# A two-layer hybrid block on one core: reciprocal roots with intermediates in PSUM, other forms of two small softmax steps, and refitted costs in the list schedule

## The chip, the cores and the metric

The kernel runs on one core of a Trainium2 chip. Times are device microseconds of an execution. The core has TensorE (PE in the rows; PEld is its weight load), VectorE (DVE), ScalarE (ACT), GpSimd (POOL) and SyncE (SP), which issues the DMAs. Each works through its own list of instructions in order and waits on semaphores for the others.

## The reference

Two layers of a block over 1024 tokens of width 1024. Each layer normalizes x, projects it, and runs three mixers side by side: a sparse attention with four heads whose keys are picked by a top-256 over an index score (`dsa`), a recurrent mixer with eight heads (`rwkv7`), and an attention with a compressed, a selected and a sliding-window branch (`nsa`). Then come an output projection, a second norm and a gated feed-forward layer.

```
for l in range(DEPTH):
    mod = silu(c) @ ada_w[l] + ada_b[l]
    h = rms_norm(x, norm1_g[l]) * (1.0 + sc1) + sh1
    z = h @ w_in[l]
    ...
    mixed = concatenate([o_a, o_b, o_c]) @ w_out[l]
    x = x + g1 * mixed
    h = rms_norm(x, norm2_g[l]) * (1.0 + sc2) + sh2
    gate, up = split(h @ ffn_wi[l])
    x = x + g2 * ((silu(gate) * up) @ ffn_wo[l])
```

Reciprocal square roots occur in the norms of x, in the norms of queries and keys (over 64 columns), in the rwkv unit (length of kk) and in its group norm.

## The kernel before, in words

All is fp32. The tokens are worked on in two halves of 512 columns, features on the 128 partitions. `proj` (stage D) and `ffn` (stage F) of each layer and half are chains of dense matmuls: a weight tile arrives by DMA (`wraw`), ScalarE rounds it to `whi`, GpSimd subtracts to get `wlo`, and three 128x128x512 matmuls per tile make up an fp32 product. The order of these stages is D00, D01, F00, D10, F01, D11, F10, F11 (layer, half).

Beside them run, as generators: `index` and `topk` (the selection by bisection on the score's bits), `compress`, `att_worker` (blocks of 128 queries through `nsa` and `dsa`, both through `attend`), and `rw_worker` (16 units, one for each layer, pair of heads and half, each with 64x64 matmuls and the inversion of 16x16 blocks on VectorE in `invert16`, tile `dg`). Tiles are taken from pools: 50 `s` slots, 34 `d`, 8 `w` in SBUF, and in PSUM six banks `ps` and two banks `mm`. The sums and the cast of a norm (`ss`, `rb`) use the `mm` banks, the other sums (`ssk`) the `ps` banks.

The order of instructions is planned when the kernel is built. `Weave` runs the generators against a clock made of `cost_of` and decides which goes on; its `fits` refuses a step when the streams could no longer all get their tiles. The result is a record of instructions; `Program.order` then list-schedules every engine's queue: the earliest possible start goes first, ties by record number, with `Chip` as the model of the engines. In it an instruction with `port` set waits while the other of VectorE and GpSimd holds the port, and an instruction with an operand in PSUM does not set it. All of this happens ahead of the run; on the chip the lists are fixed.

`rsqrt` starts from an integer shift and does three Newton steps. Its named calls are `nex` (8 norms of x), `kex` (12 norms of keys and queries) and `ex` (16 rwkv units), on 128x128 tiles with x, u and y in one SBUF slot. The sums come from `sums`, four small matmuls into one PSUM bank; `cast` spreads the root back with matmuls. Its unnamed calls are on 8 to 32 columns. In `attend`, keys may lie in two runs of up to 512 columns; then the two row maxima (`m2`, `m` in the rows) and the two row sums (`s2`) are joined.

Nearly all instructions are issued from one line (L666), so the rows are told apart by tile names.

Of the kernel before, what the change touches and what calls it, by code (L numbers as in the profile page):

```python
# [13 lines left out]
F32 = mybir.dt.float32  # L14
# [206 lines left out]
class Weave:  # L221
# [39 lines left out]
    def touch(self, h):  # L261
        h.touches += 1
        if not self.plan:

            c = self.cur
            h.last = [c.step, h.tag, int(h.touches == 1)]
            h.scope = c.scope
            self.events.setdefault(c.scope, []).append(h.last)

    def done(self, h, t):  # L270
# [41 lines left out]
    def lifetimes(self):  # L312

        p = Plan()
        p.touches = {h.key: h.touches for h in self.tiles}
        p.last = {h.key: h.scope for h in self.tiles}
        for h in self.tiles:
            h.last[2] -= 1

        p.peak, p.need = {}, {}  # L320
        for scope, ev in self.events.items():
            peak = {}
            at = ev[-1][0]
            for step, tag, n in reversed(ev):
                while at > step:
                    p.peak[scope, at] = dict(peak)
                    at -= 1
                peak[tag] = max(0, peak.get(tag, 0) + n)
            for at in range(at, -1, -1):
                p.peak[scope, at] = dict(peak)  # L330
            for step, tag, n in ev:
                s = p.need.setdefault((scope, step), {}).setdefault(tag, [0, 0])
                s[0] += n
                s[1] = max(s)
        return p

    def fits(self, s):
        need = self.plan.need.get((s.scope, s.step), {})
        free = {tag: n - self.used.get(tag, 0) for tag, n in self.bufs.items()}
        if all(n[1] <= 0 for n in need.values()):  # L340
            return True
        if any(free[tag] < n[1] for tag, n in need.items()):
            return False

        rest = [(self.plan.peak.get((o.scope, o.step), {}), self.due.get(o.scope, {})) for o in self.live
                if o.step and o is not s]
# [4 lines left out]
        rest.append((self.plan.peak.get((s.scope, s.step + 1), {}), due))  # L351
        while rest:
            for r in rest:
                if all(n <= free[tag] for tag, n in r[0].items()):
                    for tag, n in r[1].items():
                        free[tag] += n
                    rest.remove(r)
                    break
            else:
                return False  # L360
        return True
# [60 lines left out]
def cost_of(key, name, aps, kw):  # L422
# [4 lines left out]
    if key == "V":  # L427
        more = 0.055 if len(aps) - acc - (name in ("scalar_tensor_tensor", "tensor_tensor", "tensor_tensor_scan",
                                                   "copy_predicated", "tensor_tensor_reduce")) > 2 else 0.0
        if name in ("tensor_reduce", "reduce_max", "reciprocal", "transpose", "tensor_tensor_reduce"):  # L430
            return 0.15 + n / 960.0 + (0.085 if acc else 0.0), False
        if acc or psum:
            return 0.15 + more + n / 960.0 + (0.085 if acc else 0.0), False
        if name in ("tensor_scalar", "tensor_copy", "memset"):
            return 0.15 + more + n / 1900.0, n > 1
        if name == "tensor_tensor_scan":
            return 0.17 + n / 487.0, True
        return 0.15 + more + n / 960.0, True
    if key == "S":
        return (0.16 if psum else 0.2) + n / 1200.0 + 0.09 * (len(aps) - 2), False  # L440
    if key == "G":
        if name == "tensor_tensor":
            return 0.18 + n / (461.0 if all(x.ap[1][0] for x in aps[1:]) else 590.0), True
        return 0.11 + n / 1220.0, name != "memset"
    a, b = aps[:2]
    plain = all(len(x.ap) <= 2 and x.ap[0][1] == 128 for x in (a, b))
# [33 lines left out]


class Rec:
    __slots__ = ("key", "name", "a", "k", "cost", "deps", "n", "users", "pe", "func", "port")


def spread(offset, dims, unit):
# [18 lines left out]
class Program:  # L505
# [32 lines left out]
    def add(self, key, name, a, k, aps, outs, cost, pe=None, port=False):  # L538
        r = Rec()
        r.key, r.name, r.a, r.k, r.cost, r.pe, r.port = key, name, a, k, cost, pe, port  # L540
        r.n, r.deps, r.users = len(self.recs), set(), []
        r.func = a[2] if key == "S" and name == "activation" else None
        wrote = {id(x) for x in outs}
        for ap in aps:
# [127 lines left out]
class Chip:  # L672
# [25 lines left out]
    def put(self, r, s):  # L698

        if r.key == "PE":  # L700
# [5 lines left out]
                self.stretch += 1  # L706
            part = rows[1] - rows[0] + cols[1] - cols[0] < 8
            more = 0.105 if not part and self.first else 0.0
            self.first = part
            share = 1.0 if not part else (rows[1] - rows[0]) * (cols[1] - cols[0]) / 16.0  # L710
            if self.slow:
                self.lost += c * (share if share > 0.3 else 0.3)
                c *= 2
            self.work += c if not part else c * max(0.3, share)
            for i in range(*rows):
                self.cells[i][cols[0]:cols[1]] = [s + c + more] * (cols[1] - cols[0])
            self.part = part
            self.free["PE"] = s + (0.007 if part else c + more)
            return s + c
        if r.key == "D":  # L720
            self.free["D"] = s + r.cost
# [28 lines left out]
def trace(ctx: ExitStack, tc: tile.TileContext, A, out, layers=L, plan=None, program=None):  # L750
# [24 lines left out]
    PT = {'mm':'mm','tm':'mm','ss':'mm','rb':'mm','xt':'mm','out':'mm'}  # L775
    PB = dict(ps=6,mm=2)
    wv = Weave({**SB, **PB}, plan)
    V, S, G, SY = (Timed(e, k, wv, program) for e, k in ((nc.vector, "V"), (nc.scalar, "S"), (nc.gpsimd, "G"), (nc.sync, "D")))
    PE = nc.tensor

# [6 lines left out]
    def slot(name, dt=F32):  # L787
        tag = SG.get(name, "s")
        name = nm(name)
        return wv.tile(tag, lambda tag: new("s", [128, 1024 if dt == BF16 else HF], dt, name, tag))  # L790
# [131 lines left out]
        eng.tensor_tensor(lo[:, :w], t[:, :w], hi.bitcast(F32)[:, :w], op=ALU.subtract)  # L922
        return hi, lo

    def rsqrt(src, w, scale, eps, clampmin=None, name=None):

        if name:
            m = slot(name)
            x, u, y = (m[:, i * 128:i * 128 + w] for i in range(3))
        else:  # L930
            x, u, y = (small(w, f"r{n}{w}", F32, 6 if w <= 16 else 1) for n in "xuy")
        if clampmin is None:
# [4 lines left out]
        V.tensor_scalar(i, x.bitcast(I32), 1, None, op0=ALU.logical_shift_right)  # L937
        V.tensor_scalar(y.bitcast(I32), i, -1.0, float(0x5F3759DF), op0=ALU.mult, op1=ALU.add)
        for _ in range(3):
            V.tensor_tensor(u, x, y, op=ALU.mult)  # L940
            V.scalar_tensor_tensor(u, u, -0.5, y, op0=ALU.mult, op1=ALU.mult)
            V.scalar_tensor_tensor(y, u, 1.5, y, op0=ALU.add, op1=ALU.mult)
        return y

# [374 lines left out]
    def proj(l, h, spills, get, lead=None):  # L1319
# [82 lines left out]
        def c_q(i):  # L1402
            def consume(ps):
# [7 lines left out]
                def post():  # L1411
# [7 lines left out]
                    qsq.append(i)  # L1419
                    if len(qsq) < 5:  # L1420
                        return
                    r = rsqrt(qsq[0][:, :128], 128, 1.0 / 64, 1e-6, name="kex")
                    yield r
                    ps = pst("ssk")
                    transpose(ps[:, :128], r)
# [343 lines left out]
    def attend(l, b, kind, q12, vcol, blocks, bias, s0, gate, po, st, final):  # L1769
# [10 lines left out]
        for hh in range(4):  # L1780
# [19 lines left out]
                    V.reduce_max(m2[:, i:i + 1], ps[:, d0:d0 + n], axis=AX.X)  # L1800
                    pss.append((ps[:, d0:d0 + n], n, None))
            if nr == 2:
                V.tensor_tensor(m2[:, 0:1], m2[:, 0:1], m2[:, 1:2], op=ALU.max)
            nb = small(1, "nb")
            V.tensor_scalar(nb, m2[:, 0:1], scl, -1.0, op0=ALU.mult, op1=ALU.mult)
            row = []
# [5 lines left out]
            yield nb if hh < 3 else None  # L1812
        rs = small(4, "rs")
        if nr == 2:
            V.tensor_tensor(rs, s2[:, :, 0], s2[:, :, 1], op=ALU.add)
            V.reciprocal(rs, rs)
        else:
            V.reciprocal(rs, s2[:, :, 0])
# [660 lines left out]
```

## Time and profile before

| what | value |
|---|---|
| median of 3 runs | 3543.34 us (3539.09 to 3548.75) |
| the profiled execution | 3547.71 us |
| its span, first to last instruction | 3545.9 us |
| PE busy | 3308.7 us (93%) |
| DVE busy | 2203.5 us (62%) |
| ACT busy | 1793.3 us (51%) |
| POOL busy | 1480.7 us (42%) |
| mean granted TensorE clock | 0.964 of full speed |

Busy time is what an engine spends in instructions, waits inside an instruction included. The share is over the whole span, and the stages differ: the windows below show which engine is nearly full in which stretch. A matmul's end is modelled, so the busy time of PE is not its peak work.

### The profile page before, as it was taken

Reading aid. Unit: us, or ns where it says so; the run is one execution under the profiler, and the core shown is the slowest. Engines: PE = TensorE matmul, PEld = TensorE weight load, DVE = VectorE, ACT = ScalarE, POOL = GpSimd, SP = SyncE. Lnnn points to the kernel's source line nnn. Section 1 sums busy time; section 2 is a strip of 40 time slices with the busy share of each in tenths; the row PEclk is TensorE's granted clock in tenths of the full one; section 3 lists DMA queues with packets and bytes.
Section 4 is the critical chain, followed back from the end, with each engine's and each line's share of the span. In section 5 each row is a group of like instructions: output and inputs, shape, how many; then the busy total and the mean of one; then the engine's idle time right before and its main releaser. Section 6 shows DMA issues by size and latency. Waiting matters only on the chain. (4 is left out here: it accounts for less than half of the span.)

```text
span 3545.9 us, 58688 instructions
## 1 busy us (share of the span) xinstructions
PE 3308.7 (93%) x20564; PEld 2488.7 (70%) x20564; DVE 2203.5 (62%) x5705; ACT 1793.3 (51%) x3712; POOL 1480.7 (42%) x1235
## 2 busy tenths in 40 slices
PE   7899898898999998989899999899899999999999
PEld 3646666666677776667677887667677777778887
DVE  4689766889898753698964112688878952151112
ACT  3445545675576463544564233557677564343222
POOL 2423443233344434452534554443343334445554
PEclk8999999988999999899899999999999999999999
DMA  8674355434722224454223333454222222433333
GB/s 281 187 244 132 88 155 145 129 98 138 240 74 86 81 88 137 128 170 115 82 71 111 98 96 116 139 163 142 68 66 85 73 70 82 126 103 98 97 96 98
DMA packets 354756, 425.00 MB, mean 120 GB/s; under 512 B 129686, under 2 KB 167190, under 8 KB 354460
## 3 DMA queue, kind: packets, MB, share of 16 engines
q1 hardware_dynamic: 354460, 421.25, 38.8%
q8 instruction: 162, 2.65, 0.3%
q14 instruction: 134, 1.10, 0.1%
HBM read 347.06 MB, written 60.44 MB: 115 GB/s over the span
## 5 line engine op out<-in xcount | busy, mean ns | idle before, releaser
L666 POOL TENSOR_TENSOR wlo<-wraw,whi 128x512 fp32r<-128x512 f32 (+1 forms) x808 | 1062.4, 1317 | 1439.0 <-ACT whi L666 1325.7
L666 ACT ACTIVATE whi<-wraw 128x512 fp32r<-128x512 f32 (+1 forms) x808 | 501.1, 621 | 980.5 <-PE mm L666 687.9
L666 PE MATMUL mm<-hh,whi 128*128 128x512 f32 x2144 | 869.8, 407 | 21.0 <-ACT whi L666 9.7
L666 PE MATMUL mm<-hh,wlo 128*128 128x512 f32 x2128 | 845.6, 397 | 7.4 <-POOL wlo L666 7.3
L666 PE MATMUL mm<-hl,whi 128*128 128x512 f32 x2112 | 840.2, 398 | 7.6 <-DVE hl L666 4.2
L666 PEld LDWEIGHTS mm<-hh,whi 128*128 128x128 f32 x2144 | 407.6, 190 | 138.7 <-issue 30.7
L666 PEld LDWEIGHTS mm<-hh,wlo 128*128 128x128 f32 x2128 | 404.9, 190 | 103.3 <-POOL wlo L666 12.9
L666 PEld LDWEIGHTS mm<-hl,whi 128*128 128x128 f32 x2112 | 402.4, 191 | 91.2 <-DVE hl L666 6.3
L666 DVE TENSOR_TENSOR sg<-sg,mm 128x512 f32<-128x512 f32 x87 | 59.6, 686 | 491.6 <-PE mm L666 489.8
L666 DVE SCALAR_TENSOR_TENSOR x<-mm,mod,x 128x512 f32<-128x512 f32 x232 | 173.1, 747 | 255.9 <-PE mm L666 255.0
L666 PE MATMUL mm<-acthi,whi 128*128 128x512 f32 x704 | 281.0, 404 | 10.9 <-ACT acthi L666 6.8
L666 PE MATMUL mm<-actlo,whi 128*128 128x512 f32 x704 | 277.8, 397 | 2.4 <-POOL actlo L666 2.2
L666 PE MATMUL mm<-acthi,wlo 128*128 128x512 f32 x704 | 276.4, 396 | 0.0
L666 ACT ACTIVATE p<-p,nb,rst 128x512 f32<-128x512 f32 (+3 forms) x256 | 170.6, 667 | 67.7 <-DVE nb L666 64.3
L666 ACT ACTIVATE junka<-score,tk_nt 128x512 int8<-128x512 f32 x240 | 166.1, 692 | 22.2 <-DVE tk_nt L666 18.5
L666 ACT COPY pT<-pt 128x512 f32<-128x512 f32 (+2 forms) x220 | 124.7, 585 | 97.5 <-PE pt L666 85.2
L666 PEld LDWEIGHTS mm<-acthi,whi 128*128 128x128 f32 x704 | 133.1, 190 | 50.4 <-ACT acthi L666 7.9
L666 PEld LDWEIGHTS mm<-actlo,whi 128*128 128x128 f32 x704 | 133.6, 190 | 32.4 <-POOL actlo L666 7.5
L666 PEld LDWEIGHTS mm<-acthi,wlo 128*128 128x128 f32 x704 | 133.6, 190 | 28.4 <-issue 0.9
L666 PE MATMUL pt<-c_ident,p 128*128 128x128 f32 x816 | 141.0, 285 | 11.1 <-DVE p L666 8.8
L666 PE MATMUL po<-pT,tm 128*64 128x256 f32 x816 | 133.1, 409 | 9.8 <-ACT pT L666 9.8
L666 DVE TENSOR_SCALAR p<-p,rs 128x512 f32<-128x512 f32 (+3 forms) x288 | 138.9, 538 | 1.2 <-DVE tk_tr L666 0.7
(384 smaller groups left out, 5979.6 us busy)
## 6 DMA issues: line engine op xcount, KB each, us to landing
wraw<-in_wi_dram SPq DMA_DIRECT2D x352, 256.0 KB, 2.6
ada<-in_ada_dram SPq DMA_DIRECT2D x192, 256.0 KB, 4.6
wraw<-in_win_dram SPq DMA_DIRECT2D x184, 256.0 KB, 3.1
wraw<-in_wo_dram SPq DMA_DIRECT2D x160, 256.0 KB, 2.6
x<-x SPq DMA_DIRECT2D x64, 256.0 KB, 4.1
w<-in_w_dram SPq DMA_DIRECT2D x64, 256.0 KB, 3.8
wraw<-in_wout_dram SPq DMA_DIRECT2D x64, 256.0 KB, 2.7
o_in<-o SPq DMA_DIRECT2D x32, 256.0 KB, 3.2
```

The costliest lines, as they stand in the source:

```text
L666: getattr(engines[r.key], r.name)(*[real(x) for x in r.a], **{n: real(x) for n, x in r.k.items()})
```

## The change

The named roots keep x and u in a PSUM bank: in columns 128 to 255 and 256 to 383 of the bank their sums lie in (argument `room`; for the queries, whose sums are added up in SBUF, the bank of the last sum). Only y stays in SBUF. In each Newton step the scalar_tensor_tensor with -0.5 comes first and the plain multiply second. In `attend` the larger of two maxima is taken by a tensor_scalar with the second as a per-partition operand, and the two sums are added by a tensor_reduce.

The rest is the planner. `cost_of` gives a VectorE memset and a strided last dimension their own rates, and judges GpSimd's operands by their last dimension; `Chip.put` lets a part-array fp32 matmul hold TensorE for half its time instead of blocking the cells it uses; and `fits` counts tiles that are taken in one stream and freed in another (`keep`) as not coming back. `prio`, `h.first` and `program.weave` only record.

```
-    def rsqrt(src, w, scale, eps, clampmin=None, name=None):
+    def rsqrt(src, w, scale, eps, clampmin=None, name=None, room=None):
         if name:
-            m = slot(name)
-            x, u, y = (m[:, i * 128:i * 128 + w] for i in range(3))
+            y = slot(name)[:, :w]
+            room = room if room is not None else src
+            x, u = (bass.AP(tensor=room.tensor, offset=room.offset + 128 * i, ap=[list(room.ap[0]), [1, w]])
+                    for i in (1, 2))
...
         for _ in range(3):
-            V.tensor_tensor(u, x, y, op=ALU.mult)
-            V.scalar_tensor_tensor(u, u, -0.5, y, op0=ALU.mult, op1=ALU.mult)
+            V.scalar_tensor_tensor(u, x, -0.5, y, op0=ALU.mult, op1=ALU.mult)
+            V.tensor_tensor(u, u, y, op=ALU.mult)
             V.scalar_tensor_tensor(y, u, 1.5, y, op0=ALU.add, op1=ALU.mult)
...
-                    r = rsqrt(qsq[0][:, :128], 128, 1.0 / 64, 1e-6, name="kex")
+                    r = rsqrt(qsq[0][:, :128], 128, 1.0 / 64, 1e-6, name="kex", room=ps)
...
-                V.tensor_tensor(m2[:, 0:1], m2[:, 0:1], m2[:, 1:2], op=ALU.max)
+                V.tensor_scalar(m2[:, 0:1], m2[:, 0:1], m2[:, 1:2], None, op0=ALU.max)
...
-            V.tensor_tensor(rs, s2[:, :, 0], s2[:, :, 1], op=ALU.add)
+            V.tensor_reduce(rs, s2, axis=AX.X, op=ALU.add)
...
-        if name in ("tensor_scalar", "tensor_copy", "memset"):
+        if name == "memset":
+            return 0.07 + n / 1900.0, False
+        if name in ("tensor_scalar", "tensor_copy"):
             return 0.15 + more + n / 1900.0, n > 1
...
-        return 0.15 + more + n / 960.0, True
+        far = any(x.ap[-1][0] > 2 for x in aps)
+        return 0.15 + more + n / (600.0 if far else 960.0), True
...
-            return 0.18 + n / (461.0 if all(x.ap[1][0] for x in aps[1:]) else 590.0), True
+            return 0.18 + n / (461.0 if all(x.ap[-1][0] for x in aps[1:]) else 570.0), True
...
+            step = c if not part or r.a[1].dtype != F32 else c / 2 + (0.0 if self.first else 0.05)
+            if part and cols[1] - cols[0] == 1:
+                step = 0.014
...
-            for i in range(*rows):
-                self.cells[i][cols[0]:cols[1]] = [s + c + more] * (cols[1] - cols[0])
+            if not part or step < 0.05:
+                for i in range(*rows):
+                    self.cells[i][cols[0]:cols[1]] = [s + c + more] * (cols[1] - cols[0])
             self.part = part
-            self.free["PE"] = s + (0.007 if part else c + more)
+            self.free["PE"] = s + step + more
...
+        p.keep = {}
+        for h in self.tiles:
+            scope, step = h.first
+            if h.scope != scope:
+                for at in range(step + 1):
+                    k = p.keep.setdefault((scope, at), {})
+                    k[h.tag] = k.get(h.tag, 0) + 1
...
+        rest.sort(key=lambda r: sum(r[2].values()))
         while rest:
             for r in rest:
                 if all(n <= free[tag] for tag, n in r[0].items()):
                     for tag, n in r[1].items():
                         free[tag] += n
+                    for tag, n in r[2].items():
+                        free[tag] -= n
```

## Rows read from the trace of the kernel before

**Rows 1.** The head of the page: busy us, share and instructions of each engine

```profile
PE 3308.7 (93%) x20564; PEld 2488.7 (70%) x20564; DVE 2203.5 (62%) x5705; ACT 1793.3 (51%) x3712; POOL 1480.7 (42%) x1235
```

**Rows 2.** Span and mean granted TensorE clock of the core

```profile
core 0: 3545.9 us, clock 0.964
```

**Rows 3.** Windows: busy time of each engine, the first stretch and the sum of four

```profile
200.00:400.00 200.00, 180.11 (x1507) 118.78 (x1500) 174.09 (x543) 96.08 (x221) 67.10 (x66) 0.95 0.49 150
...
sum 1600.00, PE 1468.53 PEld 1080.90 DVE 1403.38 ACT 963.90 POOL 620.47; mean PE 367.13 PEld 270.23 DVE 350.84 ACT 240.97 POOL 155.12
```

**Rows 4.** Waits of PE: total us, times, longest

```profile
PE ss L666 <- DVE nsq L666: 15.6, 5, 5.8
...
PE rb L666 <- DVE nex L666: 12.4, 4, 4.0
...
PE S L666 <- DVE m L666: 3.7, 1, 3.7
```

**Rows 5.** Tile `ex` on DVE: durations in ns, min/median/max

```profile
L666 DVE SCALAR_TENSOR_TENSOR ex<-ex x96: 270/282/1359, 208.6 to 2721.4; 128x128 f32<-128x128 f32 x96
L666 DVE TENSOR_TENSOR ex<-ex x48: 243/284/1394, 207.7 to 2719.8; 128x128 f32<-128x128 f32 x48
L666 DVE TENSOR_SCALAR ex<-ex x32: 189/214/1318, 205.8 to 2712.9; 128x128 int32<-128x128 int32 x32
L666 DVE TENSOR_SCALAR ex<-ssk x16: 254/282/292, 205.3 to 2711.4; 128x128 f32<-128x128 f32 x16
```

**Rows 6.** Tile `kex` on DVE: durations in ns, min/median/max

```profile
L666 DVE SCALAR_TENSOR_TENSOR kex<-kex x72: 272/292/1409, 68.0 to 2363.1; 128x128 f32<-128x128 f32 x72
L666 DVE TENSOR_TENSOR kex<-kex x36: 271/290/1361, 67.7 to 2362.5; 128x128 f32<-128x128 f32 x36
L666 DVE TENSOR_SCALAR kex<-kex x24: 208/226/1217, 67.1 to 2353.3; 128x128 int32<-128x128 int32 x24
```

**Rows 7.** Timeline around 1723 us (start, duration) of POOL, then DVE

```profile
1723.08 1.30 POOL L666 TENSOR_TENSOR o<-o,f 128x512 f32<-128x512 f32 x1 [0.62 <-ACT o L666]
...
1722.60 0.74 DVE L666 SCALAR_TENSOR_TENSOR x<-mm,mod,x 128x512 f32<-128x512 f32 x1
1723.26 1.26 DVE L666 TENSOR_TENSOR ex<-ex 128x128 f32<-128x128 f32 x1
```

**Rows 8.** DVE's time on `ex`, `kex`, `nex`, sums over the four stretches

```profile
sum 1600.00, DVE 73.38; mean DVE 18.34
...
sum 1600.00, DVE 22.24; mean DVE 5.56
...
sum 1600.00, DVE 12.96; mean DVE 3.24
```

**Rows 9.** Tile `PTs` on DVE: one operand in PSUM, durations as above

```profile
L666 DVE TENSOR_TENSOR PTs<-PT,qr x64: 245/280/293, 293.3 to 2813.9; 128x128 f32<-128x128 f32 x64
```

**Rows 10.** Tile `m`: durations; busy us, mean ns; sums (stretches, whole)

```profile
L666 DVE TENSOR_SCALAR nb<-m,rst x192: 165/207/217, 205.5 to 2934.6; 128x1 f32<-128x1 f32 x192
...
L666 DVE TENSOR_TENSOR m<-m 128x1 f32<-128x1 f32 x96 | 32.9, 343 | 2.6 <-issue 1.5
...
sum 1600.00, DVE 78.19; mean DVE 19.55
...
sum 3546.00, DVE 114.19; mean DVE 114.19
```

**Rows 11.** DVE by form: busy us, mean ns, idle before

```profile
L666 DVE TENSOR_TENSOR dg<-dg 64x512 f32<-64x512 f32 x16 | 17.4, 1087 | 0.1
...
L666 DVE TENSOR_REDUCE dg<-dg 64x32 f32<-64x128 f32 x32 | 8.7, 272 | 0.3
```

**Rows 12.** Timeline of DVE, 807 to 821 us: a `nex` chain in company

```profile
807.74 0.28 DVE L666 TENSOR_SCALAR nex<-ss 128x128 f32<-128x128 f32 x1
...
820.72 0.28 DVE L666 SCALAR_TENSOR_TENSOR nex<-nex 128x128 f32<-128x128 f32 x1
```

**Rows 13.** Tile `macc` on DVE: durations in ns, min/median/max

```profile
L666 DVE SCALAR_TENSOR_TENSOR macc<-ada,silu_c,macc x84: 701/745/1855, 791.6 to 978.9; 128x512 f32<-128x512 f32 x84
```

More of the change, by code (lines that the diff above doesn't have):

```diff
@@ L267, in touch @@
             h.scope = c.scope
+            if h.touches == 1:
+                h.first = c.scope, c.step
             self.events.setdefault(c.scope, []).append(h.last)
@@ L343, in fits @@
             return False
-        rest = [(self.plan.peak.get((o.scope, o.step), {}), self.due.get(o.scope, {})) for o in self.live
-                if o.step and o is not s]
+        rest = [(self.plan.peak.get((o.scope, o.step), {}), self.due.get(o.scope, {}),
+                 self.plan.keep.get((o.scope, o.step), {})) for o in self.live if o.step and o is not s]
         due = dict(self.due.get(s.scope, {}))
@@ L350, in fits @@
             due[tag] = due.get(tag, 0) + n[0]
-        rest.append((self.plan.peak.get((s.scope, s.step + 1), {}), due))
+        rest.append((self.plan.peak.get((s.scope, s.step + 1), {}), due, self.plan.keep.get((s.scope, s.step + 1), {})))
+        rest.sort(key=lambda r: sum(r[2].values()))
         while rest:
@@ L482 @@
 class Rec:
-    __slots__ = ("key", "name", "a", "k", "cost", "deps", "n", "users", "pe", "func", "port")
+    __slots__ = ("key", "name", "a", "k", "cost", "deps", "n", "users", "pe", "func", "port", "prio")
 def spread(offset, dims, unit):
@@ L541, in add @@
         r.n, r.deps, r.users = len(self.recs), set(), []
+        r.prio = self.weave.cur.prio
         r.func = a[2] if key == "S" and name == "activation" else None
@@ L712, in put @@
                 self.lost += c * (share if share > 0.3 else 0.3)
-                c *= 2
+                c, step = c * 2, step * 2
             self.work += c if not part else c * max(0.3, share)
-            for i in range(*rows):
-                self.cells[i][cols[0]:cols[1]] = [s + c + more] * (cols[1] - cols[0])
+            if not part or step < 0.05:
+                for i in range(*rows):
+                    self.cells[i][cols[0]:cols[1]] = [s + c + more] * (cols[1] - cols[0])
             self.part = part
-            self.free["PE"] = s + (0.007 if part else c + more)
+            self.free["PE"] = s + step + more
             return s + c
@@ L777, in trace @@
     wv = Weave({**SB, **PB}, plan)
+    if program is not None:
+        program.weave = wv
     V, S, G, SY = (Timed(e, k, wv, program) for e, k in ((nc.vector, "V"), (nc.scalar, "S"), (nc.gpsimd, "G"), (nc.sync, "D")))
```

## The prediction

> **What bounds the kernel now.** I read first the head of the page, then the windows, then the two engines that matter. TensorE is busy for 3308.7 of 3545.9 us [rows 1], so it leaves 237.2 us idle, and its mean granted clock is 0.964 [rows 2], so it does without 0.036 x 3545.9 = 128 us more of full clock. These two sums are all that a change outside TensorE can win back. The matmuls themselves are not touched.
>
> The windows say where the idle time lies. Four stretches (200 to 400, 600 to 1200, 1500 to 1800, 2300 to 2800 us; 1600 us in all) have VectorE busy for 1403.4 us, 88%, and TensorE for 1468.5 us [rows 3]: 131.5 of the 237.2 idle us are there. In them attention, top-k and the rwkv units run beside the dense matmuls, and VectorE sets the pace. In the long feed-forward stretches between them TensorE hardly waits. What VectorE saves inside the four stretches can shorten the kernel; what it saves elsewhere can't.
>
> No one wait on TensorE is large. The largest group is 15.6 us (the sum matmuls of the norms, behind the squares, 5 times), the third 12.4 us (the cast of a norm's root, behind VectorE's root) [rows 4]. So there is no single stall to remove, and the work is in many small ones.
>
> **The change part by part.** *1. The named roots.* There are 36 of them: 16 `ex` (one per rwkv unit), 12 `kex` (8 keys, 4 queries), 8 `nex` (the norms). Each has 12 VectorE instructions on 128 columns before and after; the first multiply of each Newton step only changes places with the scalar_tensor_tensor. New is that x and u lie in columns 128 to 383 of the PSUM bank that holds the sums (for the queries, of the last one), so that no instruction of the chain reads two SBUF tensors.
>
> What that may save is seen in the spread. An `ex` instruction has a median of 282 ns (scalar_tensor_tensor), 284 (tensor_tensor) and 214 (the two integer tensor_scalars), but maxima near 1.36 us [rows 5]; `kex` the same [rows 6]. The timeline shows why: GpSimd runs `o<-o,f` from 1723.08 for 1.30 us, and the `ex` that starts at 1723.26 ends just behind it, 1.26 us later. The `x<-mm` before them, with an operand in PSUM, keeps its 0.74 us although GpSimd starts within it [rows 7]. So I read the excess as a wait for GpSimd's instruction to end, which an operand in PSUM avoids. Undisturbed, the 192 `ex` instructions would take 96 x 0.282 + 48 x 0.284 + 32 x 0.214 + 16 x 0.282 = 52.1 us, 0.271 each. In the four stretches 180 of them take 73.4 us [rows 8], against 180 x 0.271 = 48.8: 24.6 us of waits. The 144 `kex`, in the same way 72 x 0.292 + 36 x 0.290 + 24 x 0.226 + 8 x 0.282 + 4 x 0.226 = 40.0 us or 0.278 each (the last two terms, the first steps, taken as `ex<-ssk` and as the integer ones), have 52 in the stretches with 22.2 us [rows 8] against 14.5: 7.7 us. `nex` has 48 in the stretches with 13.0 us [rows 8], 0.27 each: no waits.
>
> What it may cost: the tensor_scalars that read x or u in PSUM. `ex<-ssk`, a tensor_scalar from PSUM, has 282 ns against 214 from SBUF [rows 5], 0.068 us more; twice per root and 23 roots in the stretches (180/12 + 52/12 + 48/12), 3.2 us. The two-operand forms should not get longer: a tensor_tensor with one operand in PSUM on 128x128 has 280 ns [rows 9], against 282 to 292 from SBUF. No row of before shows VectorE writing to PSUM. From below that is nothing; from above I take another 0.068 us for each of the 8 writes of a root, 23 x 8 x 0.068 = 12.5 us. I take nothing, since 280 ns is the nearer row.
>
> [...]
>
> *2. The small softmax steps.* The maximum of two 128x1 columns, 96 tensor_tensors, takes 32.9 us, 343 ns each [rows 10], on two columns of one element: mostly waits again. As a tensor_scalar with a per-partition column it should cost what `nb<-m,rst` costs, 207 ns [rows 10]: 96 x 0.136 = 13.1 us less. The stretches hold 78.2 of 114.2 us of this tile [rows 10], so 9.0 us there. The 24 sums of two halves on 128x4 become a tensor_reduce; a reduce of 128 elements has a mean of 272 ns [rows 11], and 24 of them would take 6.5 us in all, so I count no difference. The 20 unnamed roots (8 to 32 columns) only swap two instructions: nothing, since kinds, operands' homes and number stay.
>
> *3. The list schedule.* Every engine's order is computed from costs, so each refitted cost moves instructions everywhere. The strided products of the 16x16 inversions are an example: planned at 0.15 + 512/960 = 0.68 us, now 1.00, and the trace has 1.09 for one of the two kinds [rows 11]. That is nearer the truth, but 32 such products and 8 of `blk` are some 40 x 0.35 = 14 us of misjudged time, off TensorE's path. For part-array matmuls the old form lets two 64x64 products run at once in c each, the new one spaces them c/2: nearly the same rate. The added `keep` test only makes the planner refuse a step where tiles outlive their stream; keepers are tried last, so I expect few refusals. I count 0 for all of it, with a bound either way: a tenth of TensorE's idle time, 24 us.
>
> *The sum.* If all waits go, VectorE saves 24.6 + 7.7 + 9.0 - 3.2 = 38 us in the stretches. If every wait is only handed to the next instruction that reads two SBUF tensors, it saves nothing and pays 3.2 to 15.7. Around a root such neighbours are common: from 807.7 to 821 us a `nex` chain shares VectorE with wider instructions [rows 12]. I take half of 41.3 and pay 3.2: 17.5 us. VectorE is 88% busy there, not 100; I let 0.7 of it reach TensorE, 12 us. The clock loss is 128 us beside 237 idle us, 0.54 us for each, so 12 becomes 18. The profiled execution had 3547.7 us, 4.4 above the median of 3543.3; taken from its own time 3547.7 - 18 = 3530, or 3543.3 - 18 = 3525 as a median of runs.
>
> **The rivals.** *The waits move on.* The saved waits reappear on the neighbours, and the order changes nothing: 3543, within 11 us. For it: GpSimd is busy for 620 of the 1600 us [rows 3], and wide instructions such as `macc` wait in the same way, up to 1.86 us against a median of 0.75 [rows 13]. Against it: the planner now knows that a root's steps may run while GpSimd works, and can fill with them. Chance 0.18.
>
> *PSUM is dear.* All 11 instructions of a root pay 0.068 us: 23 x 11 x 0.068 = 17.2 of the 20.7 us are lost, and (3.5 x 0.7 x 1.5) leaves 4 us: 3539. Chance 0.07, since [rows 9] speaks against it. [...]
>
> *The held banks (slower).* A root now keeps its bank until its last instruction, not its first. A clean chain takes 12 x 0.27 = 3.3 us, and in company it takes 13 [rows 12]. Norms' sums come from a pool of two banks, the others from six. If one root in four makes TensorE wait 3.3 us for a bank, 9 x 3.3 = 30 us: 3573. It decides from the point where all banks of a pool are held while a root runs. Against it: TensorE's waits for a bank's release by VectorE are short now (3.7 us once, behind `m`) [rows 4]. Chance 0.08.
>
> *The order comes out worse (slower).* The new list puts some late operand ahead of ready matmuls in the four stretches. An eighth more of their 131.5 idle us is 16, with the clock 25: 3568. Nothing in the profile excludes it. Chance 0.12.
>
> *More than I count.* All 38 us of VectorE time reach TensorE, with the clock 57: 3486. Chance 0.10.
>
> **How the numbers follow.** The forecast (a gain of 11 to 40 us) has 0.45. A change of 0.3% is 11 us, about what a measurement can tell. Faster is 0.45 + 0.10, the same 0.18 + 0.07, slower 0.08 + 0.12. The range goes from 3490 (nearly all of the saving) to 3562 (most of a worse order); what lies outside is half of the last case, the banks and the tail of the worse order. The forecast's own range is 3503 to 3532.
>
> **What would show it.** In the new profile `ex` and `kex` should have maxima near 0.3 us rather than 1.4, with medians of 0.28 (right) or 0.35 (PSUM dear). `m<-m` should have a mean near 0.2. VectorE's total should fall by some 30 us or more; if it doesn't, the waits moved on. If TensorE's idle time in the stretches stays while VectorE's busy time falls, VectorE was not what held them. New waits of TensorE on `ssk` or `ss` tiles behind `ex`, `kex` or `nex` would show the banks. The forecast fails if the new order moves idle time by more than the 18 us I count, which nothing here bounds well.

## The result and the profile after

The changed kernel has a median of 3493.01 us (3489.09 to 3505.17, 4 runs) beside 3546.05 us for the kernel before in the same comparison. The ratio is 0.9855, interval [0.982, 0.989]: faster by 1.45%, about 51 us. The forecast was a gain of 18 us, so the sign was right, the time lies near the low end of the range, and the size was nearly three times the forecast.

The head of the page and the line of the core, after (they answer to [rows 1] and [rows 2]; instructions are now issued from L683):

```profile
PE 3276.2 (94%) x20564; PEld 2478.0 (71%) x20564; DVE 2184.3 (63%) x5705; ACT 1781.6 (51%) x3708; POOL 1494.4 (43%) x1235
core 0: 3487.3 us, clock 0.970
```

TensorE's idle time falls from 237.2 to 3487.3 - 3276.2 = 211.1 us, 26 less, and its busy time by 32.5 us; the clock that it does without falls from 128 to 0.030 x 3487.3 = 105 us. VectorE is busy for only 19.2 us less, not the 30 or more that the prediction gave as the sign that the saved waits are gone.

The roots did what was forecast. Tiles `ex` and `kex` on VectorE, after, in ns (min/median/max), to be read against [rows 5] and [rows 6]:

```profile
L683 DVE SCALAR_TENSOR_TENSOR ssk<-ssk,ex x48: 268/287/299, 203.3 to 2661.3; 128x128 f32<-128x128 f32 x48
L683 DVE TENSOR_TENSOR ssk<-ssk,ex x48: 266/286/300, 203.7 to 2661.9; 128x128 f32<-128x128 f32 x48
L683 DVE SCALAR_TENSOR_TENSOR ex<-ssk,ex x48: 271/278/293, 204.1 to 2662.4; 128x128 f32<-128x128 f32 x48
L683 DVE TENSOR_SCALAR ex<-ssk x16: 276/278/292, 202.2 to 2656.2; 128x128 int32<-128x128 int32 x16
...
L683 DVE SCALAR_TENSOR_TENSOR ssk<-ssk,kex x36: 280/290/300, 68.7 to 2299.7; 128x128 f32<-128x128 f32 x36
L683 DVE TENSOR_TENSOR ssk<-ssk,kex x36: 281/288/300, 69.1 to 2300.6; 128x128 f32<-128x128 f32 x36
```

Every maximum is 0.30 us; before, they reached 1.36 to 1.41 us. The medians of the two-operand forms stay at 278 to 290 ns although x and u are now written in PSUM; only the integer tensor_scalars pay, 278 ns for this one where it had 214.

The timeline of POOL and then of DVE, after, at 585 us shows both what was won and where it goes (start, duration):

```profile
585.53 2.51 POOL L683 TENSOR_TENSOR wlo<-wraw,whi 128x512 fp32r<-128x512 f32 x2 [6.78 <-ACT whi L683]
...
586.23 0.28 DVE L683 SCALAR_TENSOR_TENSOR ssk<-ssk,kex 128x128 f32<-128x128 f32 x1
586.43 0.41 DVE L683 TENSOR_SCALAR go<-gt 128x32 f32<-128x32 f32 x1
586.76 0.29 DVE L683 TENSOR_TENSOR ssk<-ssk,kex 128x128 f32<-128x128 f32 x1
587.09 0.28 DVE L683 SCALAR_TENSOR_TENSOR kex<-ssk,kex 128x128 f32<-128x128 f32 x1
587.29 0.81 DVE L683 TENSOR_TENSOR ga<-gx 128x32 f32<-128x32 f32 x1
```

Three steps of a root run within GpSimd's two subtractions, each in its clean time. Behind them `ga<-gx`, on 32 columns with both inputs in SBUF, takes 0.81 us and ends just behind GpSimd at 588.1. E1 below runs the same list with x and u in SBUF and shows which part of this is a wait that has changed its owner. Groups on VectorE by form, after (busy us, mean ns; `m<-m` to be read against [rows 10]):

```profile
L683 DVE TENSOR_TENSOR actlo<-sg,acthi 128x512 fp32r<-128x512 f32 x44 | 44.8, 1019 | 23.6 <-ACT acthi L683 23.6
L683 DVE TENSOR_SCALAR m<-m 128x1 f32<-128x1 f32 x96 | 19.7, 205 | 1.0
L683 DVE TENSOR_TENSOR iq<-rt,rot 64x512 f32<-64x512 f32 x16 | 19.5, 1221 | 3.9 <-POOL rot L683 3.5
...
L683 DVE TENSOR_REDUCE rs<-s 128x4 f32<-128x8 f32 x24 | 3.7, 155 | 17.8 <-ACT p L683 17.8
```

`m<-m` has the 205 ns that were costed (207), and the reduce of the two sums 155 ns where the sum had 267. But `actlo` went from 872 to 1019 ns and `iq` from 858 to 1221. That is not all passed on by the roots: with the same order and the old forms (E1) `actlo` has 951 ns and `iq` 1213 already, so nearly all of `iq`'s growth comes with the order. Over the whole kernel the instructions of tiles `ex` and `kex` went from 143.4 us to 96.4 (45.59 and 34.56 for those that name the tiles, 15.1 and 1.1 for the tensor_scalars `ssk<-ssk` and `ssk<-qss`), and `m<-m` gave 13.2: some 60 us, of which VectorE's total shows 19. How much of this the saved waits brought on themselves is read at E1 and E2.

TensorE's waits, after (total, times, longest; to be read against [rows 4]):

```profile
PE ss L683 <- DVE nsq L683: 12.6, 5, 5.1
...
PE rb L683 <- DVE nex L683: 8.5, 3, 4.1
...
PE bc L683 <- DVE ex L683: 6.7, 4, 3.1
...
PE ssk L683 <- DVE kex L683: 1.1, 2, 0.6
```

The last group looks like a bank held by a root, but the timeline shows what its matmul reads:

```profile
1495.57 0.33 PE L683 MATMUL ssk<-c_ident,kex 128*128 128x128 f32 x1 [0.64 <-DVE kex L683]
```

It is the transpose of a finished query root and waits for the root itself. Among TensorE's waits no sum's matmul stands behind a step of a root.

So where do 51 us come from? Cutting the kernel at the eight norms (the start of each norm's first `rb` matmul in TensorE's timeline) gives stretches that hold the same work in every version. The first stretch is 50 us everywhere and the last 371 to 373. Lengths in us, worked out from those starts and the spans:

| norm to norm | before | after | E1 | E2 | E3 | E9 | E10 | E11 | E12 |
|---|---|---|---|---|---|---|---|---|---|
| 1 to 2 | 325 | 325 | 341 | 327 | 324 | 323 | 326 | 326 | 334 |
| 2 to 3 | 446 | 415 | 420 | 418 | 416 | 420 | 403 | 412 | 428 |
| 3 to 4 | 593 | 576 | 580 | 582 | 586 | 592 | 590 | 591 | 577 |
| 4 to 5 | 344 | 335 | 343 | 334 | 343 | 344 | 338 | 344 | 340 |
| 5 to 6 | 464 | 464 | 466 | 466 | 459 | 462 | 466 | 462 | 461 |
| 6 to 7 | 321 | 330 | 337 | 316 | 314 | 315 | 311 | 320 | 330 |
| 7 to 8 | 630 | 620 | 625 | 645 | 626 | 624 | 623 | 632 | 630 |
| span | 3545.9 | 3487.3 | 3534.8 | 3509.7 | 3492.2 | 3501.9 | 3477.8 | 3508.1 | 3523.9 |

(E1 to E12 are the experiments below.) More than half of the gain, 31 us of 58.6 in the profiled executions, lies in one stretch, from the second norm (375 us) to the third (821 before, 790 after). Windows of that stretch, all engines, and then the matmuls that read `hh` (the input projection of layer 0's second half), of the kernel before:

```profile
475.00:625.00 150.00, 138.19 (x791) 100.01 (x790) 92.57 (x231) 68.98 (x155) 60.79 (x52) 0.98 0.53 155
...
675.00:821.00 146.00, 118.71 (x885) 86.28 (x883) 127.78 (x419) 97.89 (x249) 40.18 (x37) 0.83 0.36 108
sum 446.00, PE 394.84 PEld 287.73 DVE 340.48 ACT 257.95 POOL 165.92; mean PE 98.71 PEld 71.93 DVE 85.12 ACT 64.49 POOL 41.48
...
475.00:625.00 150.00, 84.69 (x252) 0.98 0.53 155
...
675.00:821.00 146.00, 0.00 (x0) 0.83 0.36 108
```

And the same of the changed kernel:

```profile
475.00:625.00 150.00, 143.09 (x1096) 100.82 (x1095) 125.45 (x367) 95.12 (x224) 61.68 (x58) 1.00 0.52 149
...
675.00:790.00 115.00, 101.39 (x766) 76.90 (x765) 100.64 (x309) 74.49 (x186) 40.94 (x34) 0.93 0.46 144
sum 415.00, PE 388.16 PEld 283.39 DVE 351.32 ACT 264.47 POOL 166.18; mean PE 97.04 PEld 70.85 DVE 87.83 ACT 66.12 POOL 41.54
...
475.00:625.00 150.00, 68.56 (x201) 1.00 0.52 149
...
675.00:790.00 115.00, 7.94 (x24) 0.93 0.46 144
```

Before, VectorE is busy for only 92.6 of the 150 us up to 625, while TensorE spends 84.7 us on matmuls that read `hh`. From 675 on none of these is left to fill the gaps between the attention and rwkv steps. The dense work that remains is the output projection (48.6 us of matmuls that read `ohi`), which needs the results of attention and rwkv. VectorE has 127.8 us of work in 146, TensorE 27 idle us, and the granted clock is 0.83. After, VectorE has 125.5 us in the first window, TensorE keeps `hh` work for later, and the stretch's idle time falls from 51.2 to 26.8 us. The gap shows best from 655 to 720 us, before and then after:

```profile
655.00:720.00 65.00, 46.94 (x353) 33.91 (x353) 55.50 (x193) 43.84 (x114) 16.34 (x17) 0.82 0.38 119
...
655.00:720.00 65.00, 65.00 (x571) 49.80 (x570) 52.94 (x168) 51.04 (x128) 23.56 (x18) 1.00 0.44 134
```

TensorE has 18 idle us there before and none after. VectorE's busy time in the whole stretch does not fall; it rises by 11 us. What held this stretch was the order of its work, not the sum of VectorE's.

What came earlier can be named. The third rwkv unit ends its state chain (`S<-S,NN`) at 487 us in the kernel before. Its next step takes two slots `sd` and zeroes them on GpSimd; its group norm (`gm<-y`) comes behind. The timelines of DVE and POOL, before:

```profile
487.17 0.23 DVE L666 TENSOR_TENSOR S<-S,NN 128x64 f32<-128x64 f32 x1 [1.18 <-PE S L666]
...
589.62 0.52 POOL L666 MEMSET sd<- 128x512 f32 x1 [3.97 <-DVE score L666]
...
602.70 0.68 DVE L666 TENSOR_REDUCE gm<-y 128x8 f32<-128x512 f32 x1
```

and after:

```profile
480.55 0.99 POOL L683 MEMSET sd<- 128x512 f32 x2
...
490.10 0.67 DVE L683 TENSOR_REDUCE gm<-y 128x8 f32<-128x512 f32 x1
```

Before, the unit gets its slots 100 us late, and the memset is released by VectorE's `score`, the index scoring. Two theories follow. **The plan**: the new costs let the planner give the third unit its slots in time, and the roots add a smaller part. **The forms**: the saved waits are the gain, and the order is a consequence. A rival to both is **chance**: any touch of the costs throws the order into another basin.

### The profile page after: what moved, and what is told of

It is laid out like the page before. It is cut to its first block, busy times and chain, and to the rows that moved or that the text cites. A ratio compares the mean times of both kernels' runs of the same rounds, so it can differ in the third digit from the quotient of the medians.

```text
span 3487.3 us, 58649 instructions
## 1 busy us (share of the span) xinstructions
PE 3276.2 (94%) x20564; PEld 2478.0 (71%) x20564; DVE 2184.3 (63%) x5705; ACT 1781.6 (51%) x3708; POOL 1494.4 (43%) x1235
## 5 line engine op out<-in xcount | busy, mean ns | idle before, releaser
L683 POOL TENSOR_TENSOR wlo<-wraw,whi 128x512 fp32r<-128x512 f32 (+1 forms) x808 | 1071.7, 1329 | 1354.7 <-ACT whi L683 1229.3
L683 ACT ACTIVATE whi<-wraw 128x512 fp32r<-128x512 f32 (+1 forms) x808 | 500.7, 621 | 993.9 <-PE mm L683 663.5
L683 PE MATMUL mm<-hh,whi 128*128 128x512 f32 x2144 | 873.7, 409 | 27.6 <-ACT hh L683 10.3
L683 PE MATMUL mm<-hh,wlo 128*128 128x512 f32 x2128 | 845.9, 398 | 7.5 <-POOL wlo L683 7.4
L683 PE MATMUL mm<-hl,whi 128*128 128x512 f32 x2112 | 843.0, 399 | 7.5 <-POOL hl L683 3.8
L683 PEld LDWEIGHTS mm<-hh,whi 128*128 128x128 f32 x2144 | 408.7, 191 | 143.7 <-issue 26.7
L683 PEld LDWEIGHTS mm<-hh,wlo 128*128 128x128 f32 x2128 | 406.3, 191 | 99.9 <-POOL wlo L683 11.7
L683 PEld LDWEIGHTS mm<-hl,whi 128*128 128x128 f32 x2112 | 403.8, 191 | 96.1 <-issue 8.8
L683 DVE TENSOR_TENSOR sg<-sg,mm 128x512 f32<-128x512 f32 x87 | 59.6, 685 | 478.2 <-PE mm L683 478.0
L683 DVE SCALAR_TENSOR_TENSOR x<-mm,mod,x 128x512 f32<-128x512 f32 x232 | 172.9, 747 | 258.6 <-PE mm L683 258.0
L683 PE MATMUL mm<-acthi,whi 128*128 128x512 f32 x704 | 279.4, 402 | 9.3 <-ACT acthi L683 5.0
L683 PE MATMUL mm<-actlo,whi 128*128 128x512 f32 x704 | 277.1, 396 | 2.8 <-POOL actlo L683 2.7
L683 PE MATMUL mm<-acthi,wlo 128*128 128x512 f32 x704 | 275.1, 394 | 0.0
L683 ACT ACTIVATE p<-p,nb,rst 128x512 f32<-128x512 f32 (+3 forms) x256 | 170.7, 668 | 81.7 <-DVE nb L683 80.9
L683 ACT ACTIVATE junka<-score,tk_nt 128x512 int8<-128x512 f32 x240 | 166.4, 693 | 29.0 <-DVE tk_nt L683 22.9
L683 ACT COPY pT<-pt 128x512 f32<-128x512 f32 (+2 forms) x220 | 124.9, 584 | 102.4 <-PE pt L683 96.8
L683 PEld LDWEIGHTS mm<-acthi,whi 128*128 128x128 f32 x704 | 132.6, 189 | 48.7 <-issue 8.0
L683 PEld LDWEIGHTS mm<-actlo,whi 128*128 128x128 f32 x704 | 133.0, 189 | 33.9 <-POOL actlo L683 7.6
L683 DVE TENSOR_SCALAR p<-p,rs 128x512 f32<-128x512 f32 (+3 forms) x288 | 153.7, 586 | 0.7
L683 PEld LDWEIGHTS mm<-acthi,wlo 128*128 128x128 f32 x704 | 133.0, 189 | 27.8 <-issue 0.8
L683 PE MATMUL pt<-c_ident,p 128*128 128x128 f32 x816 | 136.8, 282 | 8.9 <-DVE p L683 7.9
L683 PE MATMUL po<-pT,tm 128*64 128x256 f32 x816 | 132.6, 407 | 6.7 <-ACT pT L683 6.5
```

The costliest lines, as they stand in the source:

```text
L683: getattr(engines[r.key], r.name)(*[real(x) for x in r.a], **{n: real(x) for n, x in r.k.items()})
```

## The experiments

Ratios are to the kernel before, run on the same chip; its medians in these comparisons were 3550.65 to 3551.07 us.

**E1. The order of the changed kernel, the old forms.** Every engine keeps the changed kernel's list. Only where the operands live is put back: x and u of all 36 roots go to one SBUF scratch tile, and the two softmax steps take their old form. Planned with the new forms, run with the old:

```
+            if name in lone and 128 <= x.offset % HF < 384:
...
+                return bass.AP(tensor=h, offset=x.offset % HF - 128, ap=[[256, x.ap[0][1]], *x.ap[1:]])
...
+                    r.name, r.a, r.k = 'tensor_tensor', r.a[:3], dict(op=ALU.max)
```

> The instruction order of the changed kernel on every engine, but x and u of the 36 named roots in SBUF again (one scratch tile of 256 columns in place of the bank's columns) and the two softmax steps in their old forms. Only the operands' homes and the forms differ from the changed kernel. If the forms save what the forecast says (VectorE no longer waits for GpSimd inside the roots), this loses 15 to 40 us against the changed kernel (3508 to 3533, ratio 0.99 to 0.996), and ex and kex have maxima near 1.4 us again. If the new order alone makes the gain, it stays within 10 us of the changed kernel (ratio 0.983 to 0.988).

Measured: 3532.87 us, 0.9947 [0.9928, 0.9966]. Tile `ex` on DVE, the head of the page, and TensorE's largest wait, of this run:

```profile
L683 DVE SCALAR_TENSOR_TENSOR scratch<-scratch,ex x48: 258/285/1389, 209.3 to 2703.6; 128x128 f32<-128x128 f32 x48
L683 DVE TENSOR_TENSOR scratch<-scratch,ex x48: 257/286/1406, 209.7 to 2704.2; 128x128 f32<-128x128 f32 x48
...
PE 3294.1 (93%) x20564; PEld 2485.0 (70%) x20564; DVE 2235.4 (63%) x5705; ACT 1782.9 (50%) x3708; POOL 1497.0 (42%) x1235
...
PE bc L683 <- DVE ex L683: 16.8, 10, 6.4
```

The long instructions are back, with the same clean medians. VectorE is busy for 51.1 us more than in the changed kernel, and TensorE waits 16.8 us for `ex` where it waited 6.7. At this order the forms are worth 0.9947 - 0.9855 = 0.9% of 3550 us, about 33 us (from the two intervals, some 18 to 47).

This run also shows what becomes of the saved waits when the order does not change. The place of the timeline above, in E1, where GpSimd's two subtractions run from 600.25 to 602.83:

```profile
600.95 0.74 DVE L683 SCALAR_TENSOR_TENSOR scratch<-scratch,kex 128x128 f32<-128x128 f32 x1
601.61 1.35 DVE L683 TENSOR_SCALAR go<-gt 128x32 f32<-128x32 f32 x1
...
603.33 0.18 DVE L683 TENSOR_TENSOR ga<-gx 128x32 f32<-128x32 f32 x1
```

The root's step and `go<-gt` wait here; in the changed kernel they take 0.28 and 0.41 us, and `ga<-gx`, which now comes while GpSimd still runs, takes 0.81 in place of 0.18. So part of the wait is passed on and more of it is gone. Over the whole kernel the 432 instructions of the roots and the 120 of the two softmax steps take 219.3 us in E1 and 147.8 in the changed kernel, 72 less, and VectorE's total falls by 51: at a fixed order some 20 of 72 us come back on other instructions. And the stretch from the second norm to the third takes 420 us in E1, near the changed kernel's 415, though the roots wait again: that stretch belongs to the order.

**E2. The forms alone**: the kernel before and its planner, with the new roots and softmax steps, planned anew.

```
-            x, u, y = (m[:, i * 128:i * 128 + w] for i in range(3))
+            x, u = (bass.AP(tensor=room.tensor, offset=room.offset + 128 * i, ap=[list(room.ap[0]), [1, w]])
+                    for i in (1, 2))
```

> The kernel before with the new roots and softmax steps, the planner's costs and tests as before (the order is planned anew from them). Forms as the cause: 3505 to 3530 (ratio 0.988 to 0.995). Refitted costs as the cause: 3535 to 3557 (ratio 0.997 to 1.003). If any new order moves the time by chance: anywhere from 3490 to 3570.

Measured: 3511.99 us, 0.9896 [0.9877, 0.9916]. The head of the page, of this run:

```profile
PE 3285.7 (94%) x20564; PEld 2477.9 (71%) x20564; DVE 2151.1 (61%) x5705; ACT 1796.0 (51%) x3716; POOL 1488.6 (42%) x1235
```

The same 552 instructions take 148.1 us here and 210.4 in the kernel before, 62 less, and VectorE's total falls by 52.4 us, where it fell by 19.2 with the new planner. So the time that came back in the changed kernel comes in the main with its new order.

**E3. The planner alone**: the changed kernel with the roots and softmax steps of before, planned anew.

```
-            V.scalar_tensor_tensor(u, x, -0.5, y, op0=ALU.mult, op1=ALU.mult)
-            V.tensor_tensor(u, u, y, op=ALU.mult)
+            V.tensor_tensor(u, x, y, op=ALU.mult)
+            V.scalar_tensor_tensor(u, u, -0.5, y, op0=ALU.mult, op1=ALU.mult)
```

> The refitted costs, the part-array spacing and the keep test, with the old roots and softmax steps. Refitted costs as the cause: 3495 to 3515 (ratio 0.985 to 0.991). Forms as the cause: 3535 to 3557 (0.997 to 1.003). Chance of the order: anywhere from 3490 to 3570.

Measured: 3497.69 us, 0.9855 [0.9836, 0.9873], the whole gain of the change without its forms. The head of the page, of this run:

```profile
PE 3284.3 (94%) x20564; PEld 2477.4 (71%) x20564; DVE 2197.5 (63%) x5705; ACT 1779.6 (51%) x3704; POOL 1482.0 (42%) x1235
```

E2 gives 37 us and E3 51 us, and together they give 51: the parts do not add, and on top of the new planner the forms add nothing that shows (from the two intervals, 14 us either way). The table says why. E2, E3 and the changed kernel each win 28 to 31 us in the same stretch, and that can be won once. The roots of E3 wait as before: `ex` and `kex` take 76.51 + 65.28 = 141.8 us there, against 143.4 before. E1 runs the same forms in another order: VectorE is busy for 2235.4 us there and for 2197.5 in E3, and E1 is slower by 35 us in the medians. So it seems that long roots cost little where the order was made for them, and more where it was made for short ones.

**E4, E7, E8. Chance**: one constant of the planner moved by a little, VectorE's overhead from 0.078 to 0.077 in the changed kernel (E4) and in the kernel before (E7), TensorE's latency from 0.21 to 0.211 in the kernel before (E8).

```
-OVER = {"V": 0.078, "S": 0.05, "G": 0.04}
+OVER = {"V": 0.077, "S": 0.05, "G": 0.04}
...
-LAT = {"PE": 0.21, "V": 0.05, "S": 0.06, "G": 0.06, "D": 0.0}
+LAT = {"PE": 0.211, "V": 0.05, "S": 0.06, "G": 0.06, "D": 0.0}
```

> The changed kernel with one constant of the planner moved by 1 ns (VectorE's overlap between two instructions, 0.077 for 0.078 us): no cost is nearer the truth, only ties fall otherwise and the order differs. If the gain comes from better durations or from the forms, this stays within 0.3% of the changed kernel (3483 to 3503, ratio 0.982 to 0.988). If the order's chance is as large as the gain, it lies 0.5% or more away from it.

> The kernel before with VectorE's overlap in the planner at 0.077 in place of 0.078 us: no cost nearer the truth, another order. If the refit is the cause, this stays at the time before (ratio 0.997 to 1.003). If the order before was a poor draw, it gains 0.7% or more (0.985 to 0.993).

> The kernel before with TensorE's latency to its readers in the planner at 0.211 in place of 0.210 us, a second order of the same kind. Expected as for the first nudge: 0.997 to 1.003 if the refit is the cause, 0.985 to 0.993 if the order before was a poor draw.

Measured: E4 3499.81 us, 0.9857 [0.9839, 0.9876]; E7 3544.07 us, 0.9977 [0.9963, 0.999]; E8 3548.28 us, 0.9992 [0.9981, 1.0004]. Nudged orders stay within 0.23% of what they come from. The third group norm stays late in E7 and E8 (605.8 and 605.5 us) and early in E4 (493.7 us). Chance of this size does not make 1.4%. A larger push of a cost that brings it no nearer the truth was not tried, so the theory falls for small touches alone. Single stretches move more than the whole: from the kernel before to E8 the stretch from the second norm to the third shrinks by 10 us (446.3 to 436.3), and from the changed kernel to E4 that from the fourth to the fifth grows by 14 (334.8 to 348.8). Differences of that size in the table say little.

Over all fourteen profiles the third group norm and the stretch go together: where it starts by 509 us, the stretch takes 403 to 429 us; where it starts at 600 us or later (before, E6, E7, E8), 436 to 446.

**E5, E6. The planner's halves**: the kernel before with only the new `cost_of`, or only the new `Chip.put`.

```
+        far = any(x.ap[-1][0] > 2 for x in aps)
+        return 0.15 + more + n / (600.0 if far else 960.0), True
...
+            step = c if not part or r.a[1].dtype != F32 else c / 2 + (0.0 if self.first else 0.05)
```

> The kernel before with nothing new but the refitted durations of VectorE and GpSimd in the planner (strided operands, memset, GpSimd's broadcast). If better durations of these engines make the planner's gain, it gets most of it: 3495 to 3515 (ratio 0.985 to 0.991). If the spacing of part-array matmuls makes it: 0.997 to 1.003. If the order before was a poor draw, any new draw is faster: 0.985 to 0.993.

> The kernel before with nothing new but the planner's spacing of part-array matmuls on TensorE (half a duration each, cells not blocked). If this makes the gain: ratio 0.985 to 0.991. If the durations of VectorE and GpSimd make it: 0.997 to 1.003. If the order before was a poor draw: 0.985 to 0.993.

Measured: E5 3525.41 us, 0.9928 [0.9909, 0.9948], third group norm at 507.2 us. E6 3539.83 us, 0.9962 [0.9949, 0.9976], third group norm at 600.1 us. The costs clear the stall; the model of part-array matmuls does not, and gives 0.4% without that. Neither lies where it was expected: E5 gets about half of the planner's gain, not most of it (0.9928 is only in the range given to a poor draw), and E6 gains a little more than its range of 0.997 to 1.003. No run has the `keep` count alone, so its part is not shown.

**E9. The slots taken earlier.** The kernel before, planner and forms untouched: the unit takes and zeroes its slots ahead of the state chain, not behind it.

```
+        sd = [slot("sd"), slot("sd")]
+        for i in range(2):
+            G.memset(sd[i], 0.0)
...
-        sd = [slot("sd"), slot("sd")]
         for i in range(2):
-            G.memset(sd[i], 0.0)
```

> The kernel before, with one move: the two small slots `sd` of the state unit are taken and zeroed by POOL ahead of the state chain and not behind it. Theory A, a slot-starved third unit is what costs the stretch between the second and the third norm: the third group norm, which starts at 602.7 us before and at 490.1 us with the change, starts near 500 us, the stretch from the second to the third norm (446 us before, 415 us with the change) shortens by about 25 us, and the ratio to before is 0.990 to 0.995. Rival, the slot is only the last of several things late, or the planner's order decides: the third group norm stays near 600 us and the ratio between 0.997 and 1.003.

Measured: 3505.81 us, 0.988 [0.986, 0.9899], a little more than expected. POOL and DVE in the timeline, then the stretch from the second norm to the third in windows:

```profile
444.81 0.98 POOL L666 MEMSET sd<- 128x512 f32 x2
...
483.20 0.68 DVE L666 TENSOR_REDUCE gm<-y 128x8 f32<-128x512 f32 x1
...
475.00:625.00 150.00, 141.13 (x1055) 98.69 (x1053) 125.97 (x381) 94.81 (x219) 59.03 (x52) 0.97 0.51 148
...
675.00:791.00 116.00, 100.34 (x756) 71.48 (x753) 98.73 (x284) 67.37 (x162) 40.73 (x34) 0.96 0.48 154
sum 416.00, PE 382.88 PEld 275.25 DVE 346.29 ACT 257.82 POOL 167.19; mean PE 95.72 PEld 68.81 DVE 86.57 ACT 64.45 POOL 41.80
```

The group norm comes at 483 us, VectorE's first window fills to 126.0 us as in the changed kernel, and 26.7 of the 44.0 us by which the span falls are in that stretch. The plan was made anew, so other orders moved too, but of the other stretches none changed by more than 6 us. Three moved lines give most of what the change gives.

**E11. The strided rate alone**: the kernel before, with only the new duration of strided operands in `cost_of`.

```
+        far = any(x.ap[-1][0] > 2 for x in aps)
-        return 0.15 + more + n / 960.0, True
+        return 0.15 + more + n / (600.0 if far else 960.0), True
```

> The kernel before, its planner's cost of VectorE changed in one point only: strided operands are costed at the new duration; chip model, forms and all other costs as before. If the strided durations carry what the new costs alone gave (0.9928), the third group norm starts near 507 us and the ratio is 0.991 to 0.995. Rival, the part-array durations or the other costs carry it: the ratio is 0.997 to 1.003 and the group norm stays near 600 us.

Measured: 3510.4 us, 0.9894 [0.9876, 0.9912], more than expected and more than the whole new `cost_of` (E5). POOL and DVE in its timeline:

```profile
473.58 0.53 POOL L667 MEMSET sd<- 128x512 f32 x1 [4.62 <-PE tm L667]
474.81 0.53 POOL L667 MEMSET sd<- 128x512 f32 x1 [0.71 <-DVE S L667]
...
483.51 0.69 DVE L667 TENSOR_REDUCE gm<-y 128x8 f32<-128x512 f32 x1 [5.48 <-ACT y L667]
```

The second memset is released by the unit's own state chain (`S`) and the first by a `tm` matmul, neither any longer by the scoring. The stretch shortens by 34.8 us; the sum of all the others changes by 3.

**E12. The roots put back alone**: as E1, but with the new softmax steps.

```
-                if r.name == 'tensor_scalar' and r.k.get('op0') == ALU.max and isinstance(r.a[2], bass.AP):
-                    r.name, r.a, r.k = 'tensor_tensor', r.a[:3], dict(op=ALU.max)
```

> The changed kernel's order and its new softmax steps, with only the two intermediates of the roots put back in an SBUF scratch tile. If the roots are the direct saving of the new forms, the ratio to before is near that of the run with both forms put back (0.9947): 0.993 to 0.996. If the softmax steps matter too, it lies nearer to the changed kernel's 0.9855: 0.986 to 0.991.

Measured: 3524.32 us, 0.9925 [0.9899, 0.9952], between the two ranges and nearer the first. At this order the roots carry 0.9925 - 0.9855 = 0.7%, 25 us of the 33 (from the two intervals, some 9 to 40). The remaining 0.2% of the softmax steps lies within the intervals and is not shown.

**E10. Both.** The same three moved lines in the changed kernel.

```
+        sd = [slot("sd"), slot("sd")]
+        for i in range(2):
+            G.memset(sd[i], 0.0)
```

> The same move of the two slots `sd`, made in the changed kernel. If the new order had already removed the stall (group norm at 490.1 us there), nothing is left to win: the ratio to before stays between 0.983 and 0.988, as the changed kernel's 0.9855. If the later units are still held by such slots, it falls below 0.982 and this is a version that beats both.

Measured: 3481.04 us (3479.51 to 3484.42), 0.9808 [0.9791, 0.9825]: faster than both kernels, by about 70 us and 12 us in the medians (17 us from the changed kernel by the ratios, with the two intervals some 3 to 30). The line of its core:

```profile
core 0: 3477.8 us, clock 0.973
```

The third group norm moves only from 490.1 to 485.1 us, so this is not the same stall taken away a second time. By the table it wins 12 us in the stretch from 2 to 3 and 19 from 6 to 7, and loses 13 from 3 to 4. Changes of 10 to 14 us come with the small touches of E4 and E8 too, and which order makes these was not taken apart.

## Why the prediction was right, and where its size was off

**The roots: right in mechanism.** The excess was a wait for GpSimd that an operand in PSUM avoids: the maxima are 0.30 us, and E1, with the same order and x and u in SBUF, has 1.37 to 1.41 us again in `ex` and `kex`. The costs were right too: no charge for writes to PSUM by the two-operand forms, 64 ns for an integer tensor_scalar of `ex` (278 ns from PSUM, 214 from SBUF before; 68 costed). The rival "PSUM is dear", by which all 11 instructions of a root pay 0.068 us, did not come about: the two-operand rows that write to PSUM have 286 to 290 ns, and the same instructions with SBUF in its place 284 to 291 ns in E1.

**The step from VectorE to the end: the estimate was low for a fixed order.** The prediction took half of 41.3 us, paid 3.2, and came to 18 us. At the changed kernel's own order the forms save 51 us on VectorE and about 33 us at the end. So the saving on VectorE was put too low, 17.5 us, since E1 shows some 20 of 72 us passed on where the sum took half. What of it reaches the end was put too high: 18 from 17.5 is about 1, and 33 from 51 is 0.65. The clock's share was about right: E1 (clock 0.966) has 240.7 idle us on TensorE against 211.1, and some 16 us more of lost clock, 0.53 for each idle us. The four stretches of [rows 3] were too narrow a net: the kernel has 65.0 us of `kex` against 40.0 undisturbed, 25 us of waits, where the stretches show 7.7.

**"I count 0 for all of it, with a bound either way": this is the term that was mis-sized.** The list schedule alone gives 51 us (E3), twice the bound of 24. The prediction named the strided products as a cost nearer the truth, and dismissed them as "off TensorE's path". E11 shows that this one rate is worth 1.06%, in one stretch. A planner's cost need not be on the critical path to matter: it decided who got the slots. The bound was a tenth of TensorE's idle time, and no row gave the tenth; the one stretch held more (51 idle us, 27 of them between 675 and 821). That stretch also holds what the prediction missed when it wrote that there is "no single stall to remove": a unit that starts its next step 100 us late shows in no single wait of TensorE. That the time fell inside the range is in part luck: its low end, 3490, stood for nearly all of VectorE's saving, and the 51 us came from a term put at nothing.

**The rivals.** *The waits move on*: partly, and the sign given for it, VectorE's total, does not tell it from a new order. Of the 60 us saved in `ex`, `kex` and `m<-m`, 41 are back in other instructions; with the planner of before some 10 of 62 come back (E2), and at a fixed order some 20 of 72 (E1). *The held banks*: not seen among TensorE's waits. *The order comes out worse*: the reverse. *More than I count* gave a time within 7 us of the measured one, for another reason: not VectorE's saving alone, but the order.

**What stays open.** Why a longer strided rate lets the third unit ask for its slots before the scoring takes them was not followed through the planner's clock. Why the rest of the new costs takes back part of what the strided rate gives (E5 against E11) is open too, and so are the 26 us that the changed kernel wins from the third norm to the fifth: E3 wins 8 there, E2 20 and E10 10, so neither the forms nor the order alone accounts for them, and a small touch of a constant (E4) takes 12 of them away. The 27 us of the gain outside the one stretch have no shown cause.

## What to carry to other kernels

When a planner lays out the order, a refit of its costs is a change of the whole kernel: judge it by the idle time of the worst stretch (51 us here), not by the time misjudged (14 us by the prediction); even that is no bound, as E10's 70 us show. Look there for a stream that waits long for buffers while TensorE uses up the dense work which it will need as filler; taking the buffers a step earlier was worth nearly as much as the refit here (0.988 against 0.9855). And a part's worth depends on the order it runs in: both halves of this change won the same 30 us, and adding up their separate gains would have given 88 us where 51 were measured.

## What the runs showed of the hardware

The roots' two-operand instructions on VectorE write 128x128 results to PSUM at medians of 286 to 290 ns (`ex`, `kex`), beside 284 to 291 ns to SBUF in E1; `nex` has 299, beside 291 to 292 to SBUF in the kernel before. With only one input in SBUF they run through GpSimd's work undisturbed (maxima of 0.30 us, against 1.37 to 1.41 with both there, `ex` and `kex` in E1). A removed wait for GpSimd comes back in part on the next instructions that can wait, and how much depends on the order: some 20 of 72 us at a fixed order (E1), 10 of 62 in E2, 41 of 60 in the changed kernel, where other orders are in these figures too.
